# Up projections of chunk 14 by seven products, and more low parts by accumulating DMA, in a two-layer encoder kernel

## The chip, the cores and the metric

The kernel runs on one core of one Trainium2 chip. The metric is the device time of one execution in microseconds (us); lower is better. The names of the engines are those of the profile: PE is the matrix engine (its weight loads are shown as PEld), DVE the vector engine, ACT the scalar engine, POOL the GpSimd engine, SP the engine that here only starts DMAs. SBUF is the on-chip memory, PSUM the banks into which PE accumulates, HBM the memory off the core.

## The reference

A trunk of two residual layers over 512 tokens of width 1024, all in float32. Layer 0 mixes tokens by gated linear attention, layer 1 by softmax attention; each is followed by a gated MLP. The change touches only the MLP's up projection:

```python
def conv_ffn(h, w_up, w_conv, b_conv, w_down):     # D_FF = 2816, D_MODEL = 1024
    u = h @ w_up                                   # 1024 -> 2 * 2816
    u = depthwise_conv_width_3(u, w_conv) + b_conv
    val, gate = jnp.split(u, 2, axis=-1)
    return (jax.nn.silu(gate) * val) @ w_down
...
for i in range(2):
    x = x + (gla_mixer if i == 0 else attn_mixer)(rmsnorm(x, norm_mix[i]), ...)
    x = x + conv_ffn(rmsnorm(x, norm_ffn[i]), w_up[i], w_conv[i], b_conv[i], w_down[i])
```

## The kernel before

**Split precision.** A float32 matrix is held as a high part (`wh`, `nh`, `xt`, `gu`: the value rounded to the matmul's input type) and a low part (`wl`, `nl`: the rest). One product is three matmuls: high by high, high by low, low by high.

**Weights.** SP loads a piece of 128x1024 into a buffer `raw`. ACT writes `wh` from it (L319); then DVE writes `wl` as `raw` minus `wh` (L320). The other way is `low_dma`: ACT writes `wh` (L271) and then minus the same into `wl` (L272), and POOL starts a DMA that adds the original weights onto `wl` (L308). Where the original is still whole in HBM, the DMA reads it there (`wl<-in_w_up_dram`). The DMA is only put on POOL's queue at the next `flush`, which every product ends with.

**The MLP.** The 5632 outputs of the up projection go in 22 chunks (`m`) of 128 value and 128 gate outputs. A *plain* chunk (L482 to L484) takes two output tiles of 8 x 3 matmuls over 512 tokens. A chunk in the table `SEVEN` takes a two-by-two block form with seven block products instead of eight (`seven_up`): each product is 4 x 3 matmuls over 256 tokens (L1074). Its weights come in four pieces: piece 0 as loaded, piece 1 with one block replaced by a sum (L294 on DVE), piece 2 a sum of 128x1024 (`sum`, L293 on DVE), and a half piece 3 (L283 on DVE, then L285 on ACT and L286 on DVE). Between the products ACT copies partial results inside PSUM:

```python
go(1, r, True);  twice(both, r)                       # L1129, before product 6
go(6, r2, False); act.activation(r3[:, :H], r2, AF.Copy)   # L1095, before product 4
go(7, r4, True);  twice(d, r4)                        # L1129
go(4, r3[:, :H], False); go(5, r2, False)
act.activation(r3[:, H:], r2, AF.Copy)                # L1102, before product 2
add_seven(d, r3, r4)                                  # L1132 on DVE; then product 1 of the next chunk
go(2, r1, False); go(3, r2, False)
```

So a chunk runs as products 6, 7, 4, 5, then 1 of the next chunk, then its own 2 and 3. After a chunk, ACT and DVE do the convolution and the gate (L1117 to L1122), and for every two chunks below 16 the inputs of the down projection are prepared (L1138 to L1157). After chunks 9 and 17 a quarter of the down projection runs as four strips of seven products each (`down_part`), whose results POOL adds to HBM by DMA.

**Order.** The lines are issued in program order to a framework that schedules them with a cost model of its own and fixes the order on each engine when the kernel is built. At run time each engine works its row strictly in that order and waits by semaphores. Weight pieces are made up to 6 pieces ahead (`PAW`); `LOW_0` lists the chunks whose piece 0 goes by `low_dma` (in `summed`, L295 to L302).

Of the kernel before, what the change touches and what calls it, by code (L numbers as in the profile page):

```python
# [66 lines left out]
DOWN_AFTER = {9: 0, 17: 1}  # L67


SEVEN = (6, 7, 8, 10, 11, 12, 13, 15, 16, 18, 19, 20, 21)  # L70
UPA = 3
PA = 4
LOADS = 3
# [1 line left out]
INPUT_AT = {2: (0, 1), 3: (2,), 4: (3,)}  # L75
Q_DMA = ()
UP_DMA = (1, 2, 5)
LOW_0 = (7, 8)
LOW_1 = ()
LOW_2 = ()  # L80
STRIP_0 = ()
# [19 lines left out]
def hybrid_encoder_kernel(  # L101
# [74 lines left out]
    class Weights:  # L176
# [98 lines left out]
        def summed(self, src, i, h):  # L275
# [20 lines left out]
            r = self.strip[id(src), i][h]  # L296
            low = (LOW_0, LOW_1, LOW_2) if any(src is a for a in up) else (STRIP_0, (), STRIP_2)
            if i in low[h]:
# [45 lines left out]
    def add_up(layer, chunks):  # L344
        for m in chunks:
            W.add(up[layer], (m,), 4 if m in SEVEN else 2)
            if m in SEVEN and m - 1 not in SEVEN and m - 1 not in DOWN_AFTER:
                W.todo[-5:-3] = W.todo[-4], W.todo[-5]
# [668 lines left out]
    def ffn(layer, norm, cw, nxt):  # L1017
        w_dn = down_w[layer]

        ahead = {(m + i // 2, i % 2): n for m in DOWN_AFTER for i, n in ((-1, 2), (0, 2), (1, 5))}  # L1020
        ahead.update({(m - 1 + i // 2, i % 2): n for m in SEVEN for i, n in ((-1, 2), (0, 2), (1, 5))})
        plain = {}
# [18 lines left out]
        def plain_up(m):  # L1041

            pss = []
            for t in range(2):
                ps = bank("s" if t else "acc", "up")
                feature_tile(*W.half(up[layer], 2 * m + t, max(UPAW if W.wide else UPA, ahead.get((m, t), 1))), norm.hl if m < SWITCH else fresh, ps)
                pss.append(ps)
                if t == 0 and m not in DOWN_AFTER:
                    begin_up(m + 1)
                if t == 0 and m in DOWN_AFTER:  # L1050
                    down.append(down_part(DOWN_AFTER[m], m))
                    next(down[-1])
                if m == 0 and t == 0:
                    norm.tokens()
                elif m == 0:
                    norm.rows()
                    rescale()
            for t, ps in enumerate(pss):
                u = ps
                if m < SWITCH:  # L1060
                    u = tmp("u", "u")
                    dve.tensor_tensor(u, ps, norm.R, ALU.mult)
                yield t, u
# [14 lines left out]
        def begin_up(m):  # L1078
            if m in SEVEN:
                begun.append(seven_up(m))  # L1080
                next(begun[-1])

        def seven_up(m):

            pieces = {}
            go = lambda *a: product(pieces, up[layer], m, inputs, *a)
            r = bank("pt", "r1")[:, :H]
            go(1, r, True)
            both = bank("acc", "r")
            r1, r2 = both[:, :H], both[:, H:]  # L1090
            twice(both, r)
            yield
            go(6, r2, False)
            r3 = bank("s", "r3")
            act.activation(r3[:, :H], r2, AF.Copy)  # L1095
            r4 = bank("pt", "r4")[:, :H]
            go(7, r4, True)
            d = tmp("u", "u")
            twice(d, r4)
            go(4, r3[:, :H], False)  # L1100
            go(5, r2, False)
            act.activation(r3[:, H:], r2, AF.Copy)  # L1102
            add_seven(d, r3, r4)
            yield 1, d
            begin_up(m + 1)
            go(2, r1, False)
            go(3, r2, False)
            yield 0, both

        def act_up(m):  # L1110

            res = {}
            for t, u in begun.pop(0) if m in SEVEN else plain_up(m):
                cc = ((layer * 2 + t) * FC + m) * 4
# [390 lines left out]
def _layout(inputs):  # L1505
# [61 lines left out]
    seven = np.stack(quarters, 1).transpose(0, 4, 3, 1, 2, 5).reshape(2, FC, P, 4 * S)  # L1567
    a["w_up"][:, list(SEVEN)] = seven[:, list(SEVEN)]
    dn = i["ffn_w_down"].reshape(2, FC, P, KC, P)
# [29 lines left out]
```

## Time and profile before

| | |
|---|---|
| time, median of 3 runs | 1087.22 us (1086.87 to 1087.8) |
| span of the profiled execution | 1085.5 us |
| granted PE clock, mean | 1.000 |
| PE / DVE / ACT / POOL busy | 1077.5 / 888.5 / 721.1 / 136.7 us |
| bytes by DMA | 164.52 MB, mean 152 GB/s |
| MLP of layer 0, of layer 1 | about 218 to 562 us, 736 to 1085 us |

The profiled execution's own time is known by its span, from the first to the last instruction; the median of the timed runs is 1.7 us above that span. "Busy" counts the union of an engine's instructions; as matmuls overlap in a pipeline and their ends are modelled, PE reads as busy even across a delay of some tenths of a microsecond. Delays of PE are therefore read from the starts of successive matmuls.

### The profile page before, as it was taken

Reading aid. Unit: us, or ns where it says so; the run is one execution under the profiler, and the core shown is the slowest. Engines: PE = TensorE matmul, PEld = TensorE weight load, DVE = VectorE, ACT = ScalarE, POOL = GpSimd, SP = SyncE. Lnnn points to the kernel's source line nnn. Section 1 sums busy time; section 2 is a strip of 40 time slices with the busy share of each in tenths; the row PEclk is TensorE's granted clock in tenths of the full one; section 3 lists DMA queues with packets and bytes.
Section 4 is the critical chain, followed back from the end, with each engine's and each line's share of the span. In section 5 each row is a group of like instructions: output and inputs, shape, how many; then the busy total and the mean of one; then the engine's idle time right before and its main releaser. Section 6 shows DMA issues by size and latency. Waiting matters only on the chain.

```text
span 1085.5 us, 17391 instructions
## 1 busy us (share of the span) xinstructions
PE 1077.5 (99%) x6672; PEld 966.4 (89%) x6672; DVE 888.5 (82%) x1327; ACT 721.1 (66%) x1134; POOL 136.7 (13%) x153
## 2 busy tenths in 40 slices
PE   9999999999999999999999999999999999999998
PEld 8888988888999999999988888888889999999997
DVE  7998967569898899988755588666989889998882
ACT  8679575478775676666574677656877567666660
POOL 0212112021001100010015333002110010001000
PEclk9999999999999999999999999999999999999999
DMA  8744446499545633274767475549863473227542
GB/s 301 187 126 106 122 141 215 154 207 204 127 125 127 145 120 111 77 177 121 252 149 162 127 204 164 164 158 202 206 148 124 105 166 116 100 80 157 136 175 78
DMA packets 55763, 164.52 MB, mean 152 GB/s; under 512 B 6528, under 2 KB 7040, under 8 KB 55680
## 3 DMA queue, kind: packets, MB, share of 16 engines
q1 hardware_dynamic: 36192, 112.66, 32.2%
q0 software_dynamic: 14592, 42.21, 21.7%
q10 hardware_dynamic: 4896, 8.55, 2.1%
q8 instruction: 52, 0.85, 0.3%
q14 instruction: 31, 0.25, 0.1%
HBM read 114.89 MB, written 14.68 MB: 119 GB/s over the span
## 4 chain that ended last, share of the span: by engine, by line
PE 87%; DVE 6%; ACT 3%; DMA 2%; issue 2%; POOL 0%; SPq 0%; DVEq 0%; ACTq 0%; POOLq 0%
PE r L1074 37%; PE op L535 8%; PE vg L652 7%; PE up L482 4%; PE up L483 4%; PE up L484 4%; PE dn L483 2%; PE dn L484 2%; PE dn L482 2%; PE av L509 1%; PE A L482 1%; DVE wl L320 1%; PE A L484 1%; DMA nl<-xr 1%; PE B L484 1%
## 5 line engine op out<-in xcount | busy, mean ns | idle before, releaser
L320 DVE TENSOR_TENSOR wl<-raw,wh 128x1024 fp32r<-128x1024 f32 x156 | 189.8, 1220 | 31.3 <-ACT wh L319 31.1
L319 ACT ACTIVATE wh<-raw 128x1024 fp32r<-128x1024 f32 x156 | 162.6, 1053 | 73.4 <-PE op L535 20.7
L1074 PE MATMUL r<-gu,wh 128*128 128x256 f32 x896 | 161.2, 282 | 0.0
L1074 PE MATMUL r<-xt,wh 128*128 128x256 f32 x832 | 151.1, 283 | 0.4 <-ACT r L1095 0.3
L1074 PEld LDWEIGHTS r<-gu,wh 128*128 128x128 f32 x896 | 139.3, 190 | 1.0 <-ACT r L1211 0.2
L1074 PEld LDWEIGHTS r<-xt,wh 128*128 128x128 f32 x832 | 129.2, 190 | 1.6 <-ACT r L1095 1.1
L1074 PE MATMUL r<-gu,wl 128*128 128x256 f32 x448 | 126.3, 283 | 0.0
L1074 PE MATMUL r<-xt,wl 128*128 128x256 f32 x416 | 117.2, 283 | 0.0
L1074 PE MATMUL r<-nh,wh 128*128 128x256 f32 x312 | 88.8, 285 | 0.3 <-ACT r L1102 0.3
L1074 PE MATMUL r<-nh,wl 128*128 128x256 f32 x312 | 88.2, 283 | 0.0
L1074 PE MATMUL r<-nl,wh 128*128 128x256 f32 x312 | 87.9, 282 | 0.0
L1074 PEld LDWEIGHTS r<-gu,wl 128*128 128x128 f32 x448 | 85.1, 190 | 0.0
L1074 PEld LDWEIGHTS r<-xt,wl 128*128 128x128 f32 x416 | 79.1, 190 | 0.0
L482 PE MATMUL up<-nh,wh 128*128 128x512 f32 x192 | 75.3, 392 | 0.0
L483 PE MATMUL up<-nl,wh 128*128 128x512 f32 x192 | 75.2, 392 | 0.0
L484 PE MATMUL up<-nh,wl 128*128 128x512 f32 x192 | 75.2, 392 | 0.0
L535 PE MATMUL op<-oT,wh 128*128 128x512 f32 x256 | 72.4, 393 | 0.0
L271 ACT ACTIVATE wh<-raw 128x1024 fp32r<-128x1024 f32 x36 | 38.0, 1056 | 38.2 <-PE up L483 11.5
L1074 PEld LDWEIGHTS r<-nh,wh 128*128 128x128 f32 x312 | 59.3, 190 | 2.9 <-ACT r L1102 2.6
L1074 PEld LDWEIGHTS r<-nl,wh 128*128 128x128 f32 x312 | 59.4, 190 | 0.2
L1074 PEld LDWEIGHTS r<-nh,wl 128*128 128x128 f32 x312 | 59.4, 190 | 0.0
L535 PEld LDWEIGHTS op<-oT,wh 128*128 128x128 f32 x256 | 47.4, 188 | 9.7 <-ACT oT L937 0.3
(299 smaller groups left out, 2761.6 us busy)
## 6 DMA issues: line engine op xcount, KB each, us to landing
raw<-in_w_up_dram SPq DMA_DIRECT2D x84, 512.0 KB, 4.6
raw<-in_w_down_dram SPq DMA_DIRECT2D x44, 512.0 KB, 3.7
wl<-raw POOLq DMA_DIRECT2D x20, 512.0 KB, 5.3
wl<-in_w_up_dram POOLq DMA_DIRECT2D x16, 512.0 KB, 7.8
ring<-p ACTq DMA_DIRECT2D x32, 256.0 KB, 2.6
xw<-in_xw_dram SPq DMA_DIRECT2D x8, 512.0 KB, 6.6
raw<-in_w_v_dram SPq DMA_DIRECT2D x8, 512.0 KB, 5.9
raw<-in_w_g_dram SPq DMA_DIRECT2D x8, 512.0 KB, 4.0
```

Source lines behind the costliest of these rows:

```text
L271: act.activation(hi, r, AF.Copy)
L319: act.activation(hi[:, sl], a, AF.Copy)
L320: dve.tensor_tensor(lo[:, sl], a, hi[:, sl].bitcast(F32), ALU.subtract)
L482: mm(ps, wh, mh, start=start, stop=False)
L483: mm(ps, wh, ml, start=False, stop=False)
L484: return mm(ps, wl, mh, start=False, stop=stop)
L509: mm(ps[j][:, :width], hl[k][i == 2][:, j * P : (j + 1) * P], (wl if i == 1 else wh)[:, sl], start=k == 0 and i == 0, stop=k == KC - 1 and ...
L535: mm(pss[ng][n], wt[:, sl], mv, start=k == late[0][0] and i == 0, stop=k == late[-1][-1] and i == 2)
L652: last = mm(ps[j], m[:, js], w[:, sl], start=i in (1, 7, 2) and p == 0 and a == 0, stop=i in (4, 2, 3) and p == 3 and a == 2, skip_group_c ...
L1074: mm(dst, w[:, sl], m, start=start and j == 0 and a == 0, stop=j == len(pairs) - 1 and a == 2, skip_group_check=True)
```

## The change

Chunk 14 of each layer joins `SEVEN`, and the host lays its weights out accordingly. Piece 0 of chunks 11 to 16 goes by `low_dma` with the weights read from HBM; chunks 7 and 8 did so before. Nothing else is edited.

```diff
-SEVEN = (6, 7, 8, 10, 11, 12, 13, 15, 16, 18, 19, 20, 21)
+SEVEN = (6, 7, 8, 10, 11, 12, 13, 14, 15, 16, 18, 19, 20, 21)
 ...
-LOW_0 = (7, 8)
+LOW_0 = (7, 8, 11, 12, 13, 14, 15, 16)
```

Numbers behind a name tell buffers apart. On ACT in layer 0, during chunk 10 (`r682`; its copies are L1095 and L1102 into `r3692`), the row before reads:

```order
L1095 ACTIVATE r3692_3749<-r682_3683 128x256
L319 ACTIVATE wh683_3697<-sum677_3660 128x1024
L319 ACTIVATE wh678_3663<-raw664_3547 128x1024
L1129 ACTIVATE u696_3768<-r4693_3751 128x512
L319 ACTIVATE wh694_3752<-raw680_3667 128x1024
L1102 ACTIVATE r3692_3749<-r682_3683 128x256
L285 ACTIVATE wh4690_3733<-raw664_3547 128x512
L1129 ACTIVATE r704_3824<-r1698_3800 128x512
```

and the same place in the changed kernel:

```order
L1095 ACTIVATE r3692_3750<-r682_3684 128x256
L319 ACTIVATE wh683_3698<-sum677_3661 128x1024
L319 ACTIVATE wh678_3664<-raw664_3547 128x1024
L1129 ACTIVATE u696_3770<-r4693_3752 128x512
L271 ACTIVATE wh694_3753<-raw680_3668 128x1024
L272 ACTIVATE wl695_3754<-raw680_3668 128x1024
L285 ACTIVATE wh4690_3734<-raw664_3547 128x512
L1102 ACTIVATE r3692_3750<-r682_3684 128x256
L1129 ACTIVATE r704_3826<-r1698_3802 128x512
```

L272 is new, and L285 has moved ahead of L1102: two instructions stand between L271 and the copy that had none.

On ACT in layer 0, around the making of chunk 15's piece 0 (`r744` is chunk 13, `r4751` its product 7, `raw742` is piece 0 of chunk 15), the changed kernel has the rows below; before, piece 0 was an L319 alone, and its low part was DVE's.

```order
L1095 ACTIVATE r3750_4153<-r744_4100 128x256
L1129 ACTIVATE u754_4173<-r4751_4155 128x512
L319 ACTIVATE wh745_4114<-sum739_4077 128x1024
L1121 ACTIVATE y737_4072<-y737_4072 128x512
L319 ACTIVATE wh740_4080<-raw721_3941 128x1024
L271 ACTIVATE wh752_4156<-raw742_4084 128x1024
L272 ACTIVATE wl753_4157<-raw742_4084 128x1024
L1102 ACTIVATE r3750_4153<-r744_4100 128x256
```

On PE before, the place behind chunk 13's product 5 was taken by the plain chunk 14 (`up766`, its first output tile), three matmuls of which stand ahead of chunk 13's products 2 and 3 (`r743`):

```order
L1074 MATMUL r743_4093<-xt518_2617,wl723_3965 128x256
L482 MATMUL up766_4255<-nh446_2215,wh736_4028 128x512
L483 MATMUL up766_4255<-nl447_2216,wh736_4028 128x512
L484 MATMUL up766_4255<-nh446_2215,wl737_4029 128x512
L1074 MATMUL r743_4093<-nh446_2215,wh718_3932 128x256
```

In the changed kernel chunk 14 is `r762`. Directly behind its product 6 stand the first four matmuls of chunk 15's product 1 (`r1779`, with piece 0, `wh752` and `wl753`), ahead of chunk 14's products 4 and 5:

```order
L1074 MATMUL r762_4229<-xt518_2617,wl741_4081 128x256
L1074 MATMUL r1779_4351<-nh446_2215,wh752_4156 128x256
L1074 MATMUL r1779_4351<-nl447_2216,wh752_4156 128x256
L1074 MATMUL r1779_4351<-nh446_2215,wl753_4157 128x256
L1074 MATMUL r1779_4351<-nh449_2222,wh752_4156 128x256
L1074 MATMUL r3773_4299<-xt491_2434,wh734_4027 128x256
```

`wl753` is one of the pieces that now go by DMA. What moved: its first use stands 24 matmuls (products 4 and 5) ahead of the place that product 1 of a next chunk has in the code. In layer 1 the first three matmuls of product 1 stand at the same place for chunks 14 and 16, with piece 0 by DMA as well; in layer 0 the first eight of chunk 16.

## The prediction

> **What bounds the kernel now.** I read the page first, then PE's waits, then the stretch of chunks 10 to 17 by windows.
>
> ```profile
> span 1085.5 us, 17391 instructions
> PE 1077.5 (99%) x6672; PEld 966.4 (89%) x6672; DVE 888.5 (82%) x1327; ACT 721.1 (66%) x1134; POOL 136.7 (13%) x153
> PE 87%; DVE 6%; ACT 3%; DMA 2%; issue 2%; POOL 0%; SPq 0%; DVEq 0%; ACTq 0%; POOLq 0%
> ...
> PE r L1074 <- ACT r L1095: 0.3, 1, 0.3
> PE r L1074 <- ACT r L1102: 0.3, 1, 0.3
> ```
>
> PE is busy 99% and 87% of the chain that ended last; in the MLP only two waits of 0.3 us on ACT's copies show. So the change is worth what it takes off PE, less the new delays that it makes there. Who could make them is in the windows of layer 0's chunks (the columns are PE, PEld, DVE, ACT, POOL busy, the granted clock, the DMA share, GB/s):
>
> ```profile
> 390.00:400.00 10.00, 10.00 (x87) 10.00 (x86) 10.00 (x16) 8.66 (x13) 0.00 (x0) 1.00 0.50 159
> 410.00:420.00 10.00, 10.00 (x54) 8.51 (x53) 10.00 (x15) 6.90 (x11) 0.00 (x0) 1.00 0.33 107
> 420.00:430.00 10.00, 10.00 (x86) 10.00 (x85) 10.00 (x16) 8.43 (x14) 0.00 (x0) 1.00 0.25 78
> ```
>
> DVE is full from 390 us on while PE still keeps its pace: it lives on pieces made ahead. ACT has 1 to 3 us of 10 left, POOL is idle, the DMAs are at a quarter to a half. The clock is 1.00 throughout.
>
> **PE's term.** The starts of PE's matmuls around chunk 14 of layer 0, from the timeline (start, length, engine, line, instruction; here and below):
>
> ```profile
> 403.92 0.40 PE L482 MATMUL up<-nh,wh 128*128 128x512 f32 x1
> 404.61 0.38 PE L1074 MATMUL r<-nh,wh 128*128 128x256 f32 x1
> ...
> 407.58 0.40 PE L482 MATMUL up<-nh,wh 128*128 128x512 f32 x1
> ...
> 412.37 0.28 PE L1074 MATMUL r<-nh,wh 128*128 128x256 f32 x1
> ...
> 413.80 0.39 PE L482 MATMUL up<-nh,wh 128*128 128x512 f32 x1
> ...
> 419.38 0.40 PE L1074 MATMUL r<-xt,wh 128*128 128x256 f32 x2
> ```
>
> The plain chunk's 48 matmuls take 403.92 to 404.61, 407.58 to 412.37 and 413.80 to 419.38: 0.69 + 4.79 + 5.58 = 11.06 us. The 12 of a product take 412.37 to 413.80, 1.43 us. Seven products take 7 x 1.43 = 10.01 us. The change saves 1.05 us in a layer; I take the same for layer 1: **-2.1 us**. That is already the whole gain that the trace offers, and just under 0.2% of the time (2.2 us), which is about what a measurement of this kernel can tell from no change.
>
> A rule speaks against this term: the Trainium skill, TensorE: Matmul & The Clock Gate, section Back-to-back issue gap, has about 131 ns for a matmul over 512 columns in a sustained stream and 81 ns for 128. By it the plain chunk would take 6.3 us and 84 smaller matmuls at least 6.8 us, an estimate of half a microsecond lost in each layer. The rows above read 4.79 us for 21 matmuls, 228 ns each, so the measurement decides against the rule.
>
> **DVE's term.** Mean durations (the L285 row is for ACT, below), and the piece that comes nearest to its use:
>
> ```profile
> L320 DVE TENSOR_TENSOR wl<-raw,wh 128x1024 fp32r<-128x1024 f32 x156 | 189.8, 1220 | 31.3 <-ACT wh L319 31.1
> L293 DVE TENSOR_TENSOR sum<-raw,raw 128x1024 f32<-128x1024 f32 x42 | 51.2, 1218 | 0.0
> L286 DVE TENSOR_TENSOR wl<-raw,wh 128x512 fp32r<-128x512 f32 x42 | 28.9, 688 | 17.7 <-PE r L1074 17.6
> L285 ACT ACTIVATE wh<-raw 128x512 fp32r<-128x512 f32 x42 | 26.3, 627 | 7.9 <-DVE raw L283 7.7
> ...
> 394.29 1.22 DVE L320 TENSOR_TENSOR wl<-raw,wh 128x1024 fp32r<-128x1024 f32 x1
> ...
> 398.44 0.28 PE L1074 MATMUL r<-xt,wl 128*128 128x256 f32 x1
> ```
>
> Chunk 14 loses two subtractions (2.44 us) and gains the sum (1.22), pieces 1 and 2 (2.44), and four of 128x512: L294, L283, L286 and the addition L1132, at 0.69 each 2.76. That is +3.98 us; piece 0 goes by DMA. Chunks 11, 12, 13, 15 and 16 lose one subtraction each, -6.10. DVE ends 2.1 us lighter in each layer while PE ends 1.05 us lighter. The piece that comes nearest to its use, chunk 13's piece 1, ends at 395.51 for a use at 398.44: 2.9 us of cover, which three subtractions less ahead of it widen. At the end of chunk 16 the balance is 1 us better than before. So DVE costs nothing. If that cover were gone, each microsecond would land on PE.
>
> **ACT's term.** Six more copies L272 in each layer (6 x 1.05), and for chunk 14 one L319 (1.05), one L285 (0.63) and four PSUM copies (two of 0.37, two of 0.59): 9.9 us. On average ACT has room. But they stand ahead of copies for which PE waits:
>
> ```profile
> 370.10 1.05 ACT L319 ACTIVATE wh<-sum 128x1024 fp32r<-128x1024 f32 x1
> 371.05 1.05 ACT L319 ACTIVATE wh<-raw 128x1024 fp32r<-128x1024 f32 x1
> 372.00 0.59 ACT L1129 ACTIVATE u<-r 128x512 f32<-128x512 f32 x1
> 372.49 1.06 ACT L319 ACTIVATE wh<-raw 128x1024 fp32r<-128x1024 f32 x1
> 374.04 0.37 ACT L1102 ACTIVATE r<-r 128x256 f32<-128x256 f32 x1 [0.48 <-PE r L1074]
> 375.27 0.28 PE L1074 MATMUL r<-nh,wh 128*128 128x256 f32 x1
> ```
>
> L1102 now ends at 374.41, 0.86 us before PE's product 2 starts at 375.27. In the changed row L272 starts at 373.44 (0.95 behind L271, as the rows' starts are apart), L285 at 374.39, L1102 0.53 later (0.63 less the 0.1 by which neighbours overlap) at 374.92, and it ends at 375.29, when PE wants to have started: late by a few hundredths. In other chunks L272 alone stands in between, and 0.95 us less the idle of about 0.4 leaves some cover. What a late one costs is seen at chunk 7 of layer 0, where L272 stood in front of L1102 already:
>
> ```profile
> 293.32 1.05 ACT L272 ACTIVATE wl<-raw 128x1024 fp32r<-128x1024 f32 x1
> 294.28 0.36 ACT L1102 ACTIVATE r<-r 128x256 f32<-128x256 f32 x1
> 294.31 0.40 PE L1074 MATMUL r<-xt,wh 128*128 128x256 f32 x2
> 294.69 0.39 PE L1074 MATMUL r<-nh,wh 128*128 128x256 f32 x1
> ```
>
> PE's pair at 294.31 should have been followed at 294.55; it was at 294.69. Between 0 and 12 such delays of 0.15 to 0.3 us are possible, 0 to 3.6 us; I take three of 0.2: **+0.6 us**.
>
> **The DMA's term.** The low parts of chunks 7 and 8 took this from POOL's issue to landing (first layer 0, then layer 1; the last line is all 36 accumulations into `wl`), and POOL started at 278.1, 0.3 us behind the end of L272 at 277.81:
>
> ```profile
> 276.76 1.05 ACT L272 ACTIVATE wl<-raw 128x1024 fp32r<-128x1024 f32 x1
> L308 POOL DMA_DIRECT2D wl<-in_w_up_dram x2: 868/868/868, 278.1 to 294.7; - x2
> DMA to landing us min/median/max: 5.5/5.6/5.8
> L308 POOL DMA_DIRECT2D wl<-in_w_up_dram x2: 868/870/871, 800.0 to 808.4; - x2
> DMA to landing us min/median/max: 5.8/6.3/6.8
> DMA to landing us min/median/max: 4.5/6.9/9.0
> ```
>
> At the usual place of product 1 this is hidden: L272 for chunk 12 would end at 374.5 by the steps above, and chunk 12's product 1 starts near 384, 84 matmuls of 0.119 us behind chunk 11's. POOL has nothing else in its row between the two down parts, so no issue waits behind another. The 12 added transfers of 512 KB find the DMAs half idle. It is not hidden where product 1 was pulled ahead. Layer 0, chunk 15: ACT's L1129 cannot start before chunk 13's product 7 ends; it started at 401.36 before.
>
> ```profile
> 401.36 0.58 ACT L1129 ACTIVATE u<-r 128x512 f32<-128x512 f32 x1
> 398.20 0.40 PE L1074 MATMUL r<-xt,wh 128*128 128x256 f32 x2
> ```
>
> From there, by the changed row and the same spacings: the sum 401.85, the silu 402.80 (taken like L285, which has its shape), piece 1 403.33, L271 404.28, L272 405.23 to 406.28, POOL 406.6, landing at 412.1 to 413.4, at 5.8 us 412.4. PE: chunk 13's product 6 starts at 398.20. By the changed order its products 6, 7, 4 and 5, chunk 14's products 1 and 7 and chunk 13's 2 and 3 follow, 8 x 1.43 = 11.44 us; chunk 14's product 6 runs from 409.64 to 411.07, and the third matmul behind it, the first to need `wl753`, is due at 411.3. It is late by 0.8 to 2.1 us, by 1.1 at 5.8. The eight of chunk 16 then come just in time, as the first delay shifts them too. In layer 1 the pull is the same, one matmul of product 7 stands ahead and 4 or 5 more lie between, which leaves about 0.7 at chunk 14 and 0.8 at chunk 16, by the same steps. Together **+2.6 us**, between 0 (at 4.5 us, the fastest of the 36) and 5.6 (6.8 us each). The 9.0 of the slowest I leave out: the four of chunks 7 and 8 have the same size, source and place in the chunk.
>
> The Trainium skill, DMA: Bandwidth & Descriptors, section Anatomy of one DMA, gives about 2.0 us plus bytes over 436 GB/s for such a DMA, an estimate of 3.2 us for 512 KB. By it the landing would be at 409.8, ahead of its use, and the sum would be 2.6 us lower. The rows of chunks 7 and 8 read 5.5 at the least, so I go by them; the rule's case is the first rival.
>
> **Sum.** -2.1 + 0.6 + 2.6 = +1.1 us, on the profiled span 1085.5 to 1086.6. The median of the runs lies 1.7 us above the span of before, and I keep that offset: **1088.3 us**, no change that can be told.
>
> **Rivals.** *A clean gain* (0.18): the pulled matmuls find their low parts landed and the copies keep their cover. -2.1 us, 1085.1; with the small delays of the old order gone as well it may pass 0.2%. For it speaks that the DMA share is 0.25 to 0.5 in the windows above and the fastest of the 36 took 4.5; against it, that none of the four of chunks 7 and 8 landed under 5.5. *Late landings* (0.22), the one on the other side: with 6.8 us as in layer 1, each of the three places waits 1.7 to 2.1 us, 5.6 together: 1087.2 - 2.1 + 0.6 + 5.6 = 1091.3. It decides from landings of about 6.2 us on. *ACT becomes the bound* (0.10): the 9.9 us of new ACT work in 81 us meet windows that stand at 8.4 to 8.7 of 10 already; every one of the 12 copies is late by 0.3 and two pieces come late behind them: +3.6 + 2.6 - 2.1 = +4.1, 1091.3. *The gain is paid back in small change* (0.08): delays of 1 to 2 us at places not named here and none at the three, near 1087. The forecast's own case has 0.42.
>
> **Numbers.** Faster by over 0.2% is the better half of the clean gain, 0.10. Slower is late landings and the bound on ACT, 0.32. The rest is 0.58. The range takes in the clean gain at its lower end and the 1091.3 of the two others at its upper: 1085.2 to 1091.6; the likeliest case alone spans 1086.2 to 1089.4.
>
> **What would show it.** Right, if chunk 14 takes 10.0 us of matmul starts; if PE starts the third matmul of chunk 15's product 1 in layer 0 late, at the moment its `wl` lands, by 0.8 to 2.1 us; if DVE's pieces keep 3 us or more of cover. Wrong, if `wl` lands in under 5 us, if PE waits on L1102 or L1095 in most chunks, or if PE waits for a `wl` that DVE wrote.

## The result, and the profile after

| | before | after |
|---|---|---|
| time, median of 4 runs each | 1087.05 us (1086.55 to 1087.8) | 1101.91 us (1101.19 to 1103.83) |
| span of the profiled execution | 1085.5 us | 1100.2 us |
| granted PE clock, mean | 1.000 | 0.997 |
| first to last L1074 matmul of layer 0 | 251.28 us | 256.15 us |
| from there to layer 1's first L1074 | 266.55 us | 273.42 us |
| first to last L1074 matmul of layer 1 | 253.11 us | 256.29 us |

The ratio is 1.0141, 95% interval 1.0128 to 1.0155: slower by 14.9 us, far above the range. The three stretches of the table are read from the starts of these matmuls (before, then after). Like all stretches and waits below, they are those of one profiled execution of each kernel, which ran up to 1.2 us longer than the kernel's median:

```profile
279.51 0.28 PE L1074 MATMUL r<-nh,wh 128*128 128x256 f32 x1
...
530.79 0.28 PE L1074 MATMUL r<-nh,wl 128*128 128x256 f32 x1
...
797.34 0.28 PE L1074 MATMUL r<-nh,wh 128*128 128x256 f32 x1
...
1050.45 0.28 PE L1074 MATMUL r<-nh,wl 128*128 128x256 f32 x1
```

```profile
279.28 0.28 PE L1074 MATMUL r<-nh,wh 128*128 128x256 f32 x1
...
535.43 0.28 PE L1074 MATMUL r<-nh,wl 128*128 128x256 f32 x1
...
808.85 0.29 PE L1074 MATMUL r<-nh,wh 128*128 128x256 f32 x1
...
1065.14 0.28 PE L1074 MATMUL r<-nh,wl 128*128 128x256 f32 x1
```

So the products of layer 0 lose 4.9 us, those of layer 1 3.2 us, and nearly half, 6.9 us, is lost between them, where no chunk that the change names is at work. The page and PE's waits over the whole span (after):

```profile
span 1100.2 us, 17584 instructions
PE 1082.1 (98%) x6744; PEld 970.8 (88%) x6744; DVE 886.4 (81%) x1327; ACT 737.9 (67%) x1158; POOL 147.1 (13%) x165
...
PE 81%; DVE 8%; ACT 5%; DMA 3%; issue 2%; POOL 0%; SPq 0%; DVEq 0%; ACTq 0%; POOLq 0%
```

```profile
PE r L1074 <- DMA wl<-in_w_up_dram: 3.8, 4, 1.4
PE up L484 <- DMA wl<-in_w_up_dram: 3.6, 1, 3.6
...
PE r L1074 <- ACT r L1211: 0.7, 1, 0.7
...
PE r L1074 <- ACT r L1095: 0.6, 1, 0.6
...
PE r L1074 <- ACT wh L319: 0.5, 1, 0.5
PE r L1074 <- DVE wl L320: 0.5, 1, 0.5
```

DVE got lighter, by 2.1 us, and PE's share of the chain fell from 87 to 81%. One wait of 3.6 us is new at a *plain* chunk (L484). PE around it, then the same stretch by windows (columns as in the prediction):

```profile
773.48 0.39 PE L483 MATMUL up<-nl,wh 128*128 128x512 f32 x1
777.52 0.80 PE L484 MATMUL up<-xhl,wl 128*128 128x512 f32 x1 [3.65 <-DMA wl<-in_w_up_dram]
778.11 0.63 PE L482 MATMUL up<-xhl,wh 128*128 128x512 f32 x1
...
782.37 0.63 PE L483 MATMUL up<-xhl,wh 128*128 128x512 f32 x1
782.80 0.55 PE L484 MATMUL up<-xhl,wl 128*128 128x512 f32 x1
783.19 0.39 PE L482 MATMUL up<-xhl,wh 128*128 128x512 f32 x1
```

```profile
773.50:777.50 4.00, 0.37 (x2) 0.00 (x0) 4.00 (x5) 0.69 (x2) 0.00 (x0) 0.85 1.04 257
777.50:783.00 5.50, 5.48 (x13) 4.38 (x14) 2.34 (x7) 4.43 (x6) 0.86 (x1) 0.50 0.54 171
783.00:790.00 7.00, 7.00 (x32) 5.72 (x31) 6.70 (x12) 7.00 (x10) 1.73 (x2) 0.99 0.92 175
```

4.04 us pass between two starts that are normally 0.23 us apart, and the next 13 starts come 0.43 us apart at a granted clock of 0.50: 3.8 + 2.7 = 6.5 us. "PE busy" hides the second part entirely. What PE waits for is the low part of piece 1 of layer 1's chunk 2, one of the plain chunks 1, 2 and 5 whose low parts went by DMA before as well (`UP_DMA`). Its copies on ACT and its issue on POOL, first before, then after:

```profile
747.55 1.06 ACT L271 ACTIVATE wh<-raw 128x1024 fp32r<-128x1024 f32 x1 [4.38 <-PE up L483]
748.52 1.05 ACT L272 ACTIVATE wl<-raw 128x1024 fp32r<-128x1024 f32 x1
...
749.86 0.87 POOL L308 DMA_DIRECT2D wl<-in_w_up_dram  x1 [5.47 <-ACT wl L272]
```

```profile
761.58 1.05 ACT L271 ACTIVATE wh<-raw 128x1024 fp32r<-128x1024 f32 x1
...
768.27 1.04 ACT L272 ACTIVATE wl<-raw 128x1024 fp32r<-128x1024 f32 x1
...
769.61 0.87 POOL L308 DMA_DIRECT2D wl<-in_w_up_dram  x1
...
754.91 1.41 DVE L1035 SCALAR_TENSOR_TENSOR xr<-x,prm,R 128x512 f32<-128x512 f32 x2
...
757.44 1.41 DVE L1035 SCALAR_TENSOR_TENSOR xr<-x,prm,R 128x512 f32<-128x512 f32 x2
```

The high part is made 14 us later and the low part 20 us, 5 us of both because layer 0 ends later; the low part lands 7.9 us behind its issue, at 777.5. The reason, which the runs below test, is a count that the prediction never looked at. Each piece made inside the MLP takes its buffers here:

```python
def two(self):
    self.turn += self.wide
    if self.wide and self.turn % 3 == 0:          # every third piece: buffers of the residual x
        return pair("x", KC // 2, F32R, "wh"), pair("x", KC // 2, F32R, "wl")
    return pair("wh", NH, F32R, "wh"), pair("wl", NL, F32R, "wl")
```

A plain chunk calls it twice, a chunk of seven products three times (its half piece 3 lives elsewhere). With chunk 14 in `SEVEN`, all later pieces of layer 0 move by one, and layer 1 starts one further: piece 1 of its chunk 2, count 77 before, is count 78 now and falls on `x`. At that point the `x` buffers still hold the residual, until DVE's L1035 has scaled it; the first two pairs of L1035 are the DVE rows above, and the copies stand in ACT's row behind those that use its results. In the fixed order 17 matmuls of the next plain tile (769.81 to 773.48 us) stand ahead of the L484 that needs the piece. Presumably the framework's cost model saw the piece come late; its 17 matmuls did not suffice.

### The profile page after: what moved, and what is told of

Read it like the earlier page. It is cut to its first block, busy times and chain, and to the rows that moved or that the text cites. A ratio compares the mean times of both kernels' runs of the same rounds, so it can differ in the third digit from the quotient of the medians.

```text
span 1100.2 us, 17584 instructions
## 1 busy us (share of the span) xinstructions
PE 1082.1 (98%) x6744; PEld 970.8 (88%) x6744; DVE 886.4 (81%) x1327; ACT 737.9 (67%) x1158; POOL 147.1 (13%) x165
## 4 chain that ended last, share of the span: by engine, by line
PE 81%; DVE 8%; ACT 5%; DMA 3%; issue 2%; POOL 0%; SPq 0%; DVEq 0%; ACTq 0%; POOLq 0%
PE r L1074 30%; PE op L535 8%; PE vg L652 7%; PE up L484 5%; PE up L482 5%; PE up L483 5%; PE dn L483 2%; PE dn L482 2%; PE dn L484 2%; DMA wl<-in_w_up_dram 2%; DVE wl L320 1%; ACT wh L319 1%; PE av L509 1%; DVE sum L293 1%; DVE y L1118 1%
## 5 line engine op out<-in xcount | busy, mean ns | idle before, releaser
L320 DVE TENSOR_TENSOR wl<-raw,wh 128x1024 fp32r<-128x1024 f32 x144 | 175.2, 1219 | 34.7 <-ACT wh L319 34.6
L319 ACT ACTIVATE wh<-raw 128x1024 fp32r<-128x1024 f32 x144 | 150.3, 1053 | 73.7 <-PE op L535 20.7
L1074 PE MATMUL r<-xt,wh 128*128 128x256 f32 x896 | 163.9, 283 | 0.8 <-ACT r L1095 0.6
L1074 PE MATMUL r<-gu,wh 128*128 128x256 f32 x896 | 161.7, 282 | 1.3 <-ACT r L1211 0.7
L1074 PEld LDWEIGHTS r<-gu,wh 128*128 128x128 f32 x896 | 139.5, 190 | 2.7 <-ACT r L1211 1.2
L1074 PEld LDWEIGHTS r<-xt,wh 128*128 128x128 f32 x896 | 139.0, 190 | 2.2 <-ACT r L1095 1.5
L1074 PE MATMUL r<-xt,wl 128*128 128x256 f32 x448 | 125.9, 283 | 0.7 <-DVE wl L320 0.5
L1074 PE MATMUL r<-gu,wl 128*128 128x256 f32 x448 | 126.5, 283 | 0.0
L1074 PE MATMUL r<-nh,wl 128*128 128x256 f32 x336 | 95.3, 284 | 3.8 <-DMA wl<-in_w_up_dram 3.8
L1074 PE MATMUL r<-nh,wh 128*128 128x256 f32 x336 | 96.1, 286 | 0.3 <-ACT r L1102 0.2
L1074 PE MATMUL r<-nl,wh 128*128 128x256 f32 x336 | 94.7, 282 | 0.0
L1074 PEld LDWEIGHTS r<-xt,wl 128*128 128x128 f32 x448 | 84.8, 190 | 1.5 <-DVE wl L320 1.5
L1074 PEld LDWEIGHTS r<-gu,wl 128*128 128x128 f32 x448 | 85.2, 190 | 0.1
L271 ACT ACTIVATE wh<-raw 128x1024 fp32r<-128x1024 f32 x48 | 50.6, 1053 | 33.6 <-PE op L535 7.9
L1074 PEld LDWEIGHTS r<-nh,wl 128*128 128x128 f32 x336 | 64.0, 190 | 4.6 <-DMA wl<-in_w_up_dram 4.6
L1074 PEld LDWEIGHTS r<-nh,wh 128*128 128x128 f32 x336 | 63.9, 190 | 3.2 <-ACT r L1102 2.9
L1074 PEld LDWEIGHTS r<-nl,wh 128*128 128x128 f32 x336 | 64.0, 190 | 0.1
L482 PE MATMUL up<-nh,wh 128*128 128x512 f32 x160 | 62.7, 392 | 0.0
L483 PE MATMUL up<-nl,wh 128*128 128x512 f32 x160 | 62.6, 391 | 0.0
L484 PE MATMUL up<-nh,wl 128*128 128x512 f32 x160 | 62.6, 391 | 0.0
L320 DVE TENSOR_TENSOR wl<-sum,wh 128x1024 fp32r<-128x1024 f32 x44 | 53.7, 1220 | 5.7 <-ACT wh L319 5.7
```

Of the source, the lines that this page charges most:

```text
L271: act.activation(hi, r, AF.Copy)
L319: act.activation(hi[:, sl], a, AF.Copy)
L320: dve.tensor_tensor(lo[:, sl], a, hi[:, sl].bitcast(F32), ALU.subtract)
L482: mm(ps, wh, mh, start=start, stop=False)
L483: mm(ps, wh, ml, start=False, stop=False)
L484: return mm(ps, wl, mh, start=False, stop=stop)
```

## The experiments

**Each half of the change alone, and the count alone.** `seven_only`: the table `LOW_0` as before.

```diff
-LOW_0 = (7, 8, 11, 12, 13, 14, 15, 16)
+LOW_0 = (7, 8)
```

> Chunk 14 by seven products, the low parts as before (chunks 7 and 8 alone). Theory A, the shifted turn: chunk 14 makes three pieces where the plain chunk made two, so the count that sends every third piece to the x buffers stands one further in layer 1; there piece 1 of chunk 2 falls on x buffers that come free late, and PE's wait of 3.8 us at 773.5 us with the slow matmuls behind it is made by this alone. Then 1087.05 - 2.1 + 6.9 + 0 to 2 for the changed order = 1092 to 1094, with the wait still there. Theory B, late transfers: the twelve new accumulating DMAs crowd the queues and make all the waits, that one too. Then 1085 to 1087.

Measured 1100.8 us (1.0121, interval 1.0107 to 1.0134). The wait is there without one new DMA, so late transfers alone (theory B) fall as the cause; the total was missed by 7 us, mainly since layer 0's products are 6.3 us longer, worse than with the DMAs.

`low_only`: the kernel before with the new low parts and chunk 14 plain.

```diff
-LOW_0 = (7, 8)
+LOW_0 = (7, 8, 11, 12, 13, 15, 16)
```

> Chunk 14 plain as before, low parts of chunks 7, 8, 11, 12, 13, 15 and 16 by DMA. Theory A: layer 1's plain chunks run as before; what is left are waits for pulled-ahead low parts and the changed order, 2 to 5 us, 1089 to 1092. Theory B: nearly the whole loss, 10 us or more, 1097 and above, with PE's long wait early in layer 1.

Measured 1088.56 us (1.0011, 1.0002 to 1.0020): +1.1 us, even less than theory A gave it. So ten of the twelve new transfers, in their old surroundings, cost about a thirteenth of the loss.

`turn_back`: the changed kernel with the count of layer 1 as it was, up to its own chunk 14; `turn_shift`: the kernel before with `+ layer` on that line.

```diff
-                W.loads, W.wide = LOADS_FFN, 1
+                W.loads, W.wide, W.turn = LOADS_FFN, 1, W.turn - layer
```

> The changed kernel, with the count of pieces set back by one where layer 1 starts to use the x buffers, so that its pieces fall on the same kinds of buffers as before. Theory A: the wait of 3.8 us and the slow matmuls behind it go, 1101.9 - 6.9 = 1095. Theory B: no difference, 1101.9.

> The kernel before, with the count of pieces set on by one where layer 1 starts to use the x buffers; nothing else is changed. Theory A: 1087.05 + 6.9 = 1094, and the wait of 3.8 us near 770 us appears without any new DMA and without the seventh chunk. Theory B: 1087.

Measured 1092.08 us (1.0046, 1.0032 to 1.0059) and 1091.76 us (1.0042, 1.0030 to 1.0055). One unit of a buffer counter takes 9.8 us off the changed kernel, and put on the kernel before it makes the same wait (PE's waits of `turn_shift`):

```profile
PE up L484 <- DMA wl<-in_w_up_dram: 3.6, 1, 3.6
```

`turn_shift` lost 6.0 us at layer 1's start and its products came out 1.5 us shorter, so the total is below the 1094 expected; in `turn_back` the stretch before layer 1's products is back to +0.1 us and the products of layer 1 to +0.2.

`x_skip`: is it this one piece, or the shift as a whole?

```diff
-            if self.wide and self.turn % 3 == 0:
+            if self.wide and self.turn % 3 == 0 and self.turn != 78:
```

> The changed kernel, its count left shifted, but piece 1 of chunk 2 in layer 1 kept off the x buffers (it takes an ordinary pair). Theory A, the x buffers at this one piece make the early wait: 1101.9 - 6.9 = 1095, with layer 1's products still 3 us longer than before. Rival, the shifted count as a whole reorders layer 1's start: 1100 to 1102.

Measured 1097.45 us (1.0097, 1.0083 to 1.0112). The stretch before layer 1's products is back (-0.3 us), so the early wait does hang on this piece's buffers. But layer 1's products are 6.0 us longer than before, not 3, so that only 4.5 of the expected 6.9 us are won. The low parts of chunks 14 and 16, for which PE waits there, land 7.5 us behind their issue; in the changed kernel it was 6.4 and 6.0. Why they are slower is not shown.

```profile
PE r L1074 <- DMA wl<-in_w_up_dram: 6.0, 4, 2.5
```

**The low parts by DMA.** With the count of layer 1 set back, `low_less` gives those of chunks 15 and 16 back to DVE, and `split_low` issues those of 14 to 16 in two halves.

```diff
-LOW_0 = (7, 8, 11, 12, 13, 14, 15, 16)
+LOW_0 = (7, 8, 11, 12, 13, 14)
```

> The changed kernel with layer 1's count set back (1092.1), and the low parts of chunks 15 and 16 made by DVE again; 11 to 14 stay with the DMA. Theory of late landings: PE's waits for them (1.0 and 0.4 us in layer 0, 1.3 and 0.4 us in layer 1) go, 1089.0 to 1090. Rival, DVE's cover is gone: each of the four subtractions put back comes late, PE waits for a low part that DVE wrote, 1092 to 1094.

```diff
                 self.low_dma(hi, lo, r, src[i, :, : 2 * S].bitcast(F32R) if h == 0 else None)
+                if i > 13:
+                    a, b = self.pending.pop()
+                    self.pending += [(a[:, :S], b[:, :S]), (a[:, S:], b[:, S:])]
```

> The changed kernel with layer 1's count set back (1092.1), and the accumulating DMA of chunks 14, 15 and 16 issued as two of 256 KB, the half of product 1 first. Theory of late landings: product 1's half lands some 1 to 2 us earlier, PE's waits of 1.0 and 0.4 us in layer 0 and 1.3 us in layer 1 shrink to a few tenths: 1090. Rival, a landing is mostly a fixed delay: 1092, or a little more for the longer issue.

`low_less` measured 1092.18 us (1.0045, 1.0032 to 1.0057), the number of its rival: no gain over 1092.08. PE's waits for DMA are gone, but those for ACT's `wh` copies have grown from 0.5 to 1.4 us. The rival's wait, for a `wl` that DVE wrote, is not in the list; two of the three copies had themselves waited 0.2 us for DVE's L294. `split_low` measured 1089.85 us (1.0021, 1.0012 to 1.0031), 2.2 us less than `turn_back`. The order on PE, ACT and DVE is the same in both. In layer 1's chunks 14 to 16, first `turn_back`, then `split_low` (L311 is L308 there, three lines further down):

```profile
L308 POOL DMA_DIRECT2D wl<-in_w_up_dram x3: 863/863/866, 918.9 to 941.2; - x3
...
DMA to landing us min/median/max: 5.4/5.7/5.9
```

```profile
L311 POOL DMA_DIRECT2D wl<-in_w_up_dram x6: 863/1037/1211, 917.5 to 940.4; - x6
...
DMA to landing us min/median/max: 4.1/4.6/6.1
```

At the median a landing takes about 1 us less; the first half of each pair, which product 1 needs, takes 4.1 or 4.2 us. No wait for a DMA is left among PE's. This is the prediction's mechanism, and the experiment that shows its size.

**The seventh chunk without new DMAs.** `seven_back` is `seven_only` with `turn_back`'s line.

> Chunk 14 by seven products, no new low part by DMA, layer 1's count set back. Theory A: 1100.8 less the 5.6 us of layer 1's start and the 1.6 us of its products = 1093 to 1094, so that the new low parts are worth -1 to -2 us beside the seventh chunk while they cost 1.1 alone. Rival: the seventh chunk without them stalls DVE in layer 1 too as in layer 0: 1097.

Measured 1094.53 us (1.0066, 1.0052 to 1.0080). Beside the seventh chunk the new low parts are worth 2.4 us (1092.08 for 1094.53), though alone they cost 1.1. Why is in DVE's column (the third) of its windows, and in PE's waits:

```profile
400.00:410.00 10.00, 10.00 (x85) 9.98 (x84) 10.00 (x16) 7.44 (x12) 0.00 (x0) 1.00 0.27 81
410.00:420.00 10.00, 10.00 (x86) 10.00 (x86) 10.00 (x14) 7.24 (x11) 0.00 (x0) 1.00 0.30 103
420.00:430.00 10.00, 9.70 (x82) 9.49 (x80) 10.00 (x18) 6.46 (x12) 0.00 (x0) 1.00 0.26 82
```

```profile
PE r L1074 <- ACT wh L319: 5.1, 5, 1.5
```

DVE is full; ACT, named as the releaser, has idle time and copies what DVE finishes late. At the longest wait of layer 0 (PE at 431.18 us), ACT's rows are:

```profile
430.07 1.06 ACT L319 ACTIVATE wh<-sum 128x1024 fp32r<-128x1024 f32 x1 [0.44 <-DVE sum L293]
431.33 2.96 ACT L319 ACTIVATE wh<-raw 128x1024 fp32r<-128x1024 f32 x3 [0.20 <-DVE raw L294]
```

The plain chunk 14 had been DVE's breathing space: for its weights DVE made two subtractions against 11 us of PE.

**Layer 0's rest.** In `comp15` the changed kernel has the count set back at piece 0 of chunk 15 in both layers. `split_comp` does so in layer 0 alone, with `split_low`'s edit and layer 1's count as before; `all_zero` is `split_comp` with layer 1's count begun at 0.

```diff
+            self.turn -= (i, h) == (15, 0)      # with "and src is up[0]" in split_comp and all_zero
             hi, lo = self.two()
             r = self.strip[id(src), i][h]
```

> The changed kernel with the count of pieces set back by one at piece 0 of chunk 15, in both layers: all pieces from piece 1 of chunk 15 on fall on the same kinds of buffers as before the change, in layer 0 too. Setting the count back for layer 1 alone gave 1092.1 with layer 0's chunks 4.9 us longer than before. Theory A: what is late in layer 0 behind chunk 14 (1.5 us in down part 1 at 470 us, 0.6 to 1 us at 424 to 429 us) also comes from the shifted buffers: 1092.1 - 2 = 1090. Theory C: layer 0's loss lies in low parts that land late and in late copies alone, whatever buffer they are in: 1092.

> The changed kernel with its three suspects taken back together: layer 1's count as before, the accumulating DMA of chunks 14 to 16 in two halves, and in layer 0 the count set back by one at piece 0 of chunk 15. Without the last of these it took 1089.85, and layer 0's products were still 3.2 us longer than before, 1.7 us of it two waits in down part 1 at 469 to 470 us. Theory A, those two come from the shifted buffers behind chunk 14: 1089.85 - 1.7 = 1088.1. Rival, the wait only moves to another place: 1089.9.

> The same, with layer 1's count begun at 0 instead, which made the kernel before 1.4 us faster. If that gain is had here too: 1088.1 - 1.4 = 1086.7. Rival, beside a seventh chunk at 14 the waits of layer 1's products stay (late copies and chunk 15's product 1): 1088 to 1089.

`comp15` measured 1092.51 us (1.0046, 1.0034 to 1.0059): layer 0's products 1.6 us shorter than in `turn_back`, but layer 1's 2.1 us longer; the two waits of down part 1 had moved from 470 us to 992 us. `split_comp` measured 1089.02 us (1.0019, 1.0010 to 1.0027), 0.9 us off theory A; the two waits were gone and another, for DVE, stood at 419.24 (L1078 and L324 are L1074 and L320, four lines further down):

```profile
419.24 0.39 PE L1078 MATMUL r<-xt,wl 128*128 128x256 f32 x1 [1.17 <-DVE wl L324]
```

`all_zero` measured 1091.55 us (1.0039, 1.0025 to 1.0053), where 1086.7 or at the worst 1089 was expected: 1.3 us of waiting for one L1102 copy and the two of down part 1 came up in layer 1. So layer 0's remaining loss is not one cause: in each of these placements its products stay some 3 us longer than before, with late copies and late pieces at other places.

Not every such wait belongs to a placement. The wait for the L1102 copy stands behind a piece that SP loads from HBM and that lands late in some executions only: at the same place the profile of `split_low` has 1.0 us and that of `split_comp` none, though the order of PE, ACT and DVE in layer 1 is the same in both. In the same way PE's start at 310 us, behind L1095, is 1.0 us late in `turn_back` and 0.2 us in `split_low`. A difference of 1 us between two stretches can thus be chance.

**The count as a knob of its own**, on the kernel before: `shift_late` adds one from chunk 6 of layer 1 on, `turn_zero` begins layer 1 at 0, and `late_low` is `shift_late` with the low parts of chunks 11, 12, 13, 15 and 16 by DMA in layer 1.

```diff
-                W.loads, W.wide = LOADS_FFN, 1
+                W.loads, W.wide, W.turn = LOADS_FFN, 1, 0        # turn_zero
...
+            self.turn += (i, h) == (6, 0) and src is up[1]      # shift_late, late_low
             hi, lo = self.two()
```

> The kernel before, with the count set on by one from chunk 6 of layer 1 on, behind the place where it cost 6 us. With the shift from chunk 2 on the stretch of layer 1's products was 1.5 us shorter than before (251.6 for 253.1 us). Theory A, each shift has a price of its own at each place: 1087.4 - 1.5 = 1085.9. Theory B, the shorter stretch only gave back what PE's early wait had cost (work made ahead meanwhile): 1087.4 or more.

> The kernel before with layer 1's count begun at 0 as in layer 0, that is one back (the third of the three places that the count can have). Piece 1 of chunk 2 takes an ordinary pair. Theory A: no early wait, layer 1's start as before; its products between 1.5 us shorter and 1 us longer, 1085.5 to 1088.5. Rival, the buffers before were picked so that every other place costs several us: 1090 or more.

> The kernel before with the count set on by one from chunk 6 of layer 1 on (1086.0), and the low parts of chunks 11, 12, 13, 15 and 16 by DMA in layer 1 alone, where they shortened the products by 0.5 us in the run with the low parts alone. If the two gains add: 1085.4. Rival, product 1 is pulled ahead there too and waits for landings: 1087 to 1088.

Measured 1085.96 us (0.9988, 0.9979 to 0.9996), 1086.13 us (0.9986, 0.9977 to 0.9995) and 1087.21 us (0.9997, 0.9989 to 1.0006). The first two beat both kernels by moving buffers alone, about 1.4 us against the runs of before beside them; their products in layer 1 take 2.6 and 1.9 us less. `shift_late` came out as its theory A had it (1085.9). In `late_low` most of the gain is lost again, as its rival had it, 0.8 us of it where PE starts product 7 of three chunks of layer 1 late.

## Why the prediction was wrong

**The step that failed** is in PE's term: "I take the same for layer 1", and with it the whole working, which cost chunks 10 to 17 of one layer and copied them. No term looked at layer 1's plain chunks, although the changed order has 17 matmuls of the next tile inside a half-finished one just there. What the runs showed in its place is a count of buffers that goes on from layer 0 into layer 1. It cost 9.8 us: 6.8 us at layer 1's start and 3.0 us in its products (`turn_back` against after), where the low parts of chunks 14 to 16 land in 6.0 to 7.6 us with the count shifted and in 5.4 to 5.9 us with it set back; why the count changes that is not shown. Without the shift in layer 1 the time is 1092.08 us, half a microsecond above the upper end of the range. So a second part of the sum was too small as well, by nearly 4 us, and the terms below show where.

**Layer 0's sum**, from PE's starts. Of the 4.9 us that its products lost, the changed kernel's late starts give these parts: low parts that land late 1.6 us (414 and 425 us), late copies of ACT 0.9 us, one late load 0.7 us (310 us), two waits in down part 1 at 471 and 472 us 1.5 us. Those two hang on the count as well: with it set back at chunk 15 they left layer 0, in `split_comp` altogether, in `comp15` to come up in layer 1. Another 1.1 us is lost in starts about 0.1 us late, most of them directly behind a late one (0.22 instead of 0.12 us apart). Less 1.0 us that PE saves, that is 4.8. The prediction had terms for the first two and the last.

**PE's term** was right as far as PE goes: chunk 14's 84 matmuls start 0.12 us apart, 10.1 us where they aren't held up, for 11.06 before. But it was paid back wholly, and more.

**DVE's term** was wrong as "costs nothing", and its balance came out at half: DVE's busy time fell by 2.1 us in all (886.4 for 888.5), where 2.1 in each layer was worked out. `seven_back` shows that without the low parts DVE is the bound behind chunk 14. In the changed kernel one wait for a DVE-written `wl` reads 0.5 us, at product 7 of layer 1's chunk 15. The weight loads show that there are four (they stand in front of their matmuls and wait for the same piece; window 800 to 1070 us):

```profile
PEld r L1074 <- DVE wl L320: 1.5, 4, 0.7
```

The four are product 7 of layer 1's chunks 12 to 15, whose first matmuls the new order has ahead of product 2 of the chunk before. The first one with a `wl` starts 0.05 us behind the end of DVE's L320, 0.2 to 0.6 us late, 1.3 us in all. "Wrong, if PE waits for a `wl` that DVE wrote" came true. In layer 0 no piece was late, but the least cover among chunks 10 to 17 fell from 2.9 us to 0.4 us. The 2.9 us had been read at the old order's uses, and the new order uses such pieces earlier.

**ACT's term** was 0.6 us between 0 and 3.6, and right in kind. In layer 0 three starts are late by 0.9 us together (366, 376 and 408 us), and at each of them L272, or L272 and L285, stands directly in front of the copy (L1102, or L1211, its like in the down parts), as worked out. That is inside the bounds and, for one layer alone, already above the estimate. A fourth start, behind L1095 at 310 us, is 0.7 us late, but behind a piece that came late from HBM.

**The DMA's term** held best. The third matmul of chunk 15's product 1 in layer 0:

```profile
413.05 0.28 PE L1074 MATMUL r<-nl,wh 128*128 128x256 f32 x1
414.25 0.39 PE L1074 MATMUL r<-nh,wl 128*128 128x256 f32 x1 [0.92 <-DMA wl<-in_w_up_dram]
...
424.93 0.39 PE L1074 MATMUL r<-nh,wl 128*128 128x256 f32 x1 [0.40 <-DMA wl<-in_w_up_dram]
...
933.55 0.39 PE L1074 MATMUL r<-nh,wl 128*128 128x256 f32 x1 [1.44 <-DMA wl<-in_w_up_dram]
...
956.27 0.39 PE L1074 MATMUL r<-nh,wl 128*128 128x256 f32 x1 [1.02 <-DMA wl<-in_w_up_dram]
```

1.20 us from start to start less the usual 0.12 is 1.1 us late, as worked out, at a landing of 5.7 us against the 5.8 taken; issue and use both came 1.9 us later than worked out, so that their distance held. Chunk 16 was 0.6 us late instead of just in time, and layer 1's two places 1.6 and 1.2 instead of 0.7 and 0.8, as their landings took 6.4 and 6.0 us. 4.4 us in all against the 2.6 forecast, under the bound of 5.6. Halving these transfers, with the count of layer 1 set back, gave 2.2 us back. The Trainium skill (DMA: Bandwidth & Descriptors, Anatomy of one DMA) has a DMA through GpSimd as a fixed 2.0 us plus bytes over 436 GB/s, an estimate of 3.2 us for the whole and 2.6 us for a half: the direction agrees, both sizes are well below the 5.7 and 4.6 us measured.

**Of the rivals**, late landings was nearest in sign and mechanism. None of them, and no condition that was to prove the prediction wrong, named a wait in a chunk that the change doesn't name.

## What to carry to other kernels

When a change alters how many buffers, pieces or names are drawn in one stage, follow every counter and rotation that carries over into later stages, and compare the order of the whole program, the untouched half first. A breather in a stage where a second engine is full may be what keeps the first engine busy: shortening it is worth only what the second engine can follow. And a piece whose landing or making has 3 us of cover at its usual place has none once its first use is pulled ahead, so cover is to be taken from the changed order.

## What the runs showed of the hardware

A wait of PE can cost 1.7 times its length (6.5 us for 3.8). Behind the 4.0 us without a matmul the granted clock stood at 0.50 for 5.5 us (13 matmuls of 512 columns 0.43 us apart, 2.7 us lost). The Trainium skill (TensorE: Matmul & The Clock Gate, HAM oscillation — how this bites in real kernels) has gaps of more than about 3.4 us halve the clock, and this row agrees. `x_skip` shows that a shorter gap can do it too, and need not: 2.8 us between two starts were followed by a clock of 0.50, and the same 25 us later by 1.00. What decides between the two is not shown:

```profile
924.00:927.00 3.00, 0.57 (x5) 0.37 (x4) 3.00 (x5) 1.53 (x4) 0.00 (x0) 0.98 0.71 212
927.00:930.00 3.00, 2.90 (x13) 2.91 (x14) 2.96 (x4) 1.89 (x2) 0.00 (x0) 0.50 0.04 18
...
949.50:952.30 2.80, 0.35 (x4) 0.15 (x2) 2.80 (x5) 1.54 (x4) 0.00 (x0) 1.00 0.66 203
952.30:956.00 3.70, 3.67 (x31) 3.67 (x31) 3.67 (x5) 3.23 (x5) 0.00 (x0) 1.00 0.45 158
```
